# A conditioned decoder block in one kernel: order of the opening, place of the rotary tables, pace of the modulation, order at the second norm

## The chip, the cores and the metric

One NeuronCore of a Trainium2 chip runs the whole kernel. The metric is device time in microseconds. The engines are TensorE (PE, matmuls; PEld, its weight loads), VectorE (DVE), ScalarE (ACT), GpSimd (POOL) and SyncE (SP, which here only issues DMAs). Each engine works through its own queue in order; an instruction that waits holds up all that stands behind it on its queue.

## The reference

One decoder block on x of 256 tokens by 2048 channels, batch 1, float32 throughout:

```python
mod = (silu(c) @ ada_w + ada_b)            # 6 vectors of 2048: shift, scale, gate of mixer and of FFN
h = rmsnorm(x, norm_mix_g) * (1 + scale_m) + shift_m
x = x + gate_m * token_mix(h, cos, sin, ...)   # h @ w_in -> GLA and MLA branches, gated merge, @ w_out
h = rmsnorm(x, norm_ffn_g) * (1 + scale_f) + shift_f
x = x + gate_f * swiglu(h, ffn_w_in, ffn_w_down)
return rmsnorm(x, final_norm_g)
```

`cos` and `sin` are the rotary tables, from the positions. `ada_w` is 2048 x 12288: 100 MB that are multiplied with one vector only. The weights of the matmuls are read once each.

## The kernel before

**Matmuls.** float32 operands are split in two parts of reduced precision: `hi` is a copy on ACT (L111), `lo` the difference on DVE (L112), and each product is three matmuls (L170-172 or L180-182). Weights come in halves: 256 rows by 512 columns, 512 KB, loaded into a ring of raw buffers (`raw_tile`, six buffers plus what `more_raw` adds), split into `hi` and `lo` (three buffers each). A half gives twelve matmuls of 512 columns. After each half the program calls `tick()`.

**Modulation in the background.** `tick()` runs what is in `later`, then `background()`, which advances the generators in the list `bg` by `pace[0]` steps on the average, then one step of the attention lanes `ATT` and `GLA`. Two kinds of generator stand in `bg`: `ada_cols` (L247) takes the transposed weight of one block of 128 channels, loads four half rows of 512 KB and forms a dot product of each with the row `crow` on DVE; it ends with `modulate` (L318), which scales, shifts and splits a block of h. `ada_steps` (L270) loads 256 rows by 512 columns per step, eight steps, adds them up on DVE with two operations per step (L282, L284), and for three of the six vectors sums over partitions on GpSimd (L294); that is a ninth step. `background(1000)` at L871 runs whatever is left when the last block (`i == 3`) of the `w_out` product begins, as the FFN's norm needs those vectors.

**Stages.** Opening (L406-425): x is loaded, `crow` is broadcast with four matmuls, x is squared and transposed (`x_blocks`), the norm's factor goes through `rsqrt_mean` (eleven small DVE operations) and `rows_of` (two DVE operations, one broadcast matmul, one copy), and the blocks 0 and 1 are modulated. Then the projections: sixteen jobs (each 512 or 368 columns of `w_in`) in four rounds over the contraction (2, 4, 4 and 6 blocks of 128), while the background makes the next round's blocks of h. In round 4, after job 0, `rope_tables` (L382) makes the sine and cosine tables from the angles that `rope_angles` (L348) computes on GpSimd. Then the MLA heads in eight pairs together with three gate blocks and the GLA scores (56 ticks), the GLA output gate (L779, 32 ticks), `mla_wo` (L801, 32), `gla_wo` (L822, 32), `w_out` (L855, 32, of which 24 ahead of `i == 3`), the second norm (L897-911), the FFN (L923) and the last norm. There are 12 `ada_steps` generators between the heads and `w_out`.

**What sets the order.** The program is traced in order, but a planner, which simulates the engines, decides the order on each queue: the instruction that is ready first by its simulation goes first, so an instruction can stand far ahead of its place in the program. `keep_in_program_order(ins)` pins an instruction behind the one that was traced before it on its engine; `add_manual_dep(..., NoSync)` pins it behind a named one. Both set an order in a queue and add no wait by themselves. In the opening of before only the two loads of x are pinned.

**Lines to follow.** L407: loads of x. L408: `rope_angles`. L411-415: `crow`. L417: squares. L197-209: factor. L215-219: broadcast of the factor. L253: loads of the half rows, L256: dots. L321-323: `modulate`. L384-395: rotary tables. L728, L822, L855: paces. L871: the rest of the background. L888-890: residual add and square at `w_out`. L902-907: transposes and copies of the new x. L916, L917: two loads issued by GpSimd behind the norm.

Of the kernel before, what the change touches and what calls it, by code (L numbers as in the profile page):

```python
# [51 lines left out]
def tile_block(ctx: ExitStack, tc: tile.TileContext, x, positions, ada_w, ada_t, ada_b, w_in, gla_gk_w, gla_wo,  # L52
# [52 lines left out]
    def split_raw(raw, kk, cols, perm=None):  # L105
# [58 lines left out]
    def form_a(ps, w, ah, al, k0, first, last, cols, rows=(0, 1)):  # L164
        for kk, (hi, lo) in enumerate(w):
            k = k0 + kk
            for t in rows:
# [4 lines left out]
                T.matmul(ps[t][:, :cols], lhsT=al[:, k, ts], rhs=hi, start=False, stop=en)  # L172
# [22 lines left out]
    def rsqrt_mean(dst, ssq, n, w, eng=None):  # L195
        v, l = sb(w, "rv"), sb(w, "rl")
        V.tensor_scalar(out=v, in0=ssq, scalar1=1.0 / n, scalar2=EPS, op0=ALU.mult, op1=ALU.add)  # L197
        yi = dst.bitcast(I32)
        V.tensor_scalar(out=yi, in0=v.bitcast(I32), scalar1=-0.5, scalar2=float(0x5F3759DF), op0=ALU.mult, op1=ALU.add)
        for _ in range(3):  # L200
# [6 lines left out]
            V.tensor_tensor(out=l, in0=dst, in1=dst, op=ALU.mult)  # L207
            V.scalar_tensor_tensor(out=l, in0=l, scalar=-0.5, in1=v, op0=ALU.mult, op1=ALU.mult)
            V.scalar_tensor_tensor(out=dst, in0=l, scalar=1.5, in1=dst, op0=ALU.add, op1=ALU.mult)

    def rows_of(col, dst):
        ps = aux_bank()
        d = sb(S, "e", 3)
        for t in range(2):
            V.tensor_scalar(out=d[:, t * P:(t + 1) * P], in0=ident, scalar1=col[:, t:t + 1], scalar2=None, op0=ALU.mult)  # L215
# [31 lines left out]
    def ada_cols(k, now=False):  # L247
        for m in (1, 0):
            c = m * 16 + k
            part = sb(1, "md", 4)  # L250
            for hf in range(2):
                raw = raw_tile()
                nc.sync.dma_start(out=raw, in_=ada_t[m * D + k * P:m * D + (k + 1) * P, hf * 1024:(hf + 1) * 1024])  # L253

                def dot(raw=raw, hf=hf, c=c, part=part):
                    V.tensor_tensor_reduce(out=raw, in0=raw, in1=crow[:, hf * 1024:(hf + 1) * 1024], scale=1.0,  # L256
                                           scalar=part if hf else cb[:, c:c + 1], op0=ALU.mult, op1=ALU.add,
                                           accum_out=mod[:, c:c + 1] if hf else part)

                if now:  # L260
                    dot()
# [120 lines left out]
    def rope_tables(ang, ang2):  # L382
        four = sb(512, "sc", 2)
        V.scalar_tensor_tensor(out=ang2, in0=ang, scalar=-1.0, in1=ang, op0=ALU.mult, op1=ALU.max)  # L384
# [3 lines left out]
        for i, a in enumerate((ang, ang2)):  # L388
            A.copy(out=four[:, i * S:(i + 1) * S].rearrange("p (t r f) -> p t r f", t=2, r=4),
                   in_=a.rearrange("p (t f) -> p t f", t=2).unsqueeze(2).broadcast_to([P, 2, 4, 32]))  # L390
            for t in range(2):
                c = slice(i * S + t * P, i * S + (t + 1) * P)
                T.transpose(out=ps[:, c], in_=four[:, c], identity=ident)
        A.activation(out=sin_t, in_=ps[:, 0:S], func=AF.Sin, scale=sgn)
# [11 lines left out]
    for t in range(2):  # L406
# [642 lines left out]
```

## Time and profile before

| | us |
|---|---|
| median of 3 runs | 1770.57 (1770.28 to 1771.84) |
| profiled execution, its own time | 1769.9 |
| its span, first to last instruction | 1768.1 |
| TensorE busy | 1694.1 (96%) |
| DVE busy | 1235.1 (70%) |
| ACT busy | 832.2 (47%) |
| GpSimd busy | 121.2 (7%) |
| HBM traffic | 410.5 MB read, 6.3 MB written |

Busy shares are averages over the whole span. A timeline row reads: start, length, engine, line, operation, output and input tile with their shapes, count, and in brackets how long the engine had been idle before and what released it. A row with a count above 1 covers several instructions back to back. [...] In the code `s`, `raw`, `mm`, `aux` and so on are names of tiles; `s` stands for all large slots.

### The profile page before, as it was taken

Reading aid. Unit: us, or ns where it says so; the run is one execution under the profiler, and the core shown is the slowest. Engines: PE = TensorE matmul, PEld = TensorE weight load, DVE = VectorE, ACT = ScalarE, POOL = GpSimd, SP = SyncE. Lnnn points to the kernel's source line nnn. Section 1 sums busy time; section 2 is a strip of 40 time slices with the busy share of each in tenths; the row PEclk is TensorE's granted clock in tenths of the full one; section 3 lists DMA queues with packets and bytes.
Section 4 is the critical chain, followed back from the end, with each engine's and each line's share of the span. In section 5 each row is a group of like instructions: output and inputs, shape, how many; then the busy total and the mean of one; then the engine's idle time right before and its main releaser. Section 6 shows DMA issues by size and latency. Waiting matters only on the chain.

```text
span 1768.1 us, 23022 instructions
## 1 busy us (share of the span) xinstructions
PE 1694.1 (96%) x8388; PEld 1427.0 (81%) x8388; DVE 1235.1 (70%) x1797; ACT 832.2 (47%) x1154; POOL 121.2 (7%) x139
## 2 busy tenths in 40 slices
PE   4999999999999999999996799999999999999997
PEld 2998899889998887788884588888888888788885
DVE  5999977587786477999887767667664444555556
ACT  4644434356666555444442254444444444444443
POOL 5000000000000111110011100000000000000001
PEclk7999999999999999999998899999999999999999
DMA  8999986655545487999997658788786666555552
GB/s 300 355 349 322 322 249 195 187 190 150 171 117 187 158 297 242 357 367 317 323 345 261 238 155 273 236 251 270 237 248 189 189 191 190 178 190 187 187 186 108
DMA packets 196074, 418.31 MB, mean 237 GB/s; under 512 B 13060, under 2 KB 23636, under 8 KB 195320
## 3 DMA queue, kind: packets, MB, share of 16 engines
q1 hardware_dynamic: 194136, 410.27, 71.0%
q0 software_dynamic: 1680, 6.51, 1.0%
q8 instruction: 66, 1.08, 0.2%
q14 instruction: 48, 0.39, 0.1%
q10 hardware_dynamic: 144, 0.07, 0.0%
HBM read 410.49 MB, written 6.30 MB: 236 GB/s over the span
## 4 chain that ended last, share of the span: by engine, by line
PE 90%; DVE 4%; POOL 2%; issue 2%; DMA 1%; ACT 1%; DVEq 0%; ACTq 0%; POOLq 0%
PE mm L171 20%; PE mm L172 20%; PE mm L170 20%; PE mm L180 3%; PE mm L181 3%; PE mm L182 3%; PE mm L959 2%; PE mm L960 2%; PE mm L961 2%; PE gx L685 2%; PE gx L960 1%; PE aux L960 1%; PE aux L959 1%; PE gx L959 1%; PE aux L961 1%
## 5 line engine op out<-in xcount | busy, mean ns | idle before, releaser
L112 DVE TENSOR_TENSOR lo<-raw,hi 128x1024 fp32r<-128x1024 f32 (+3 forms) x518 | 599.7, 1163 | 356.6 <-ACT hi L111 354.3
L111 ACT CAST hi<-raw 128x1024 fp32r<-128x1024 f32 (+3 forms) x518 | 506.5, 984 | 567.6 <-PE mm L172 400.1
L171 PE MATMUL mm<-lo,s 128*128 128x512 f32 (+1 forms) x1648 | 647.1, 393 | 2.4 <-DVE lo L112 2.2
L172 PE MATMUL mm<-hi,s 128*128 128x512 f32 (+1 forms) x1648 | 640.9, 390 | 0.0
L170 PE MATMUL mm<-hi,s 128*128 128x512 f32 (+1 forms) x1648 | 587.1, 392 | 22.8 <-ACT hi L111 21.6
L170 PEld LDWEIGHTS mm<-hi,s 128*128 128x128 f32 x1648 | 310.3, 189 | 88.7 <-ACT hi L111 24.3
L171 PEld LDWEIGHTS mm<-lo,s 128*128 128x128 f32 x1648 | 311.8, 189 | 67.5 <-DVE lo L112 6.0
L172 PEld LDWEIGHTS mm<-hi,s 128*128 128x128 f32 x1648 | 311.7, 189 | 61.6 <-issue 0.7
L284 DVE SCALAR_TENSOR_TENSOR ada<-raw,cact,ada 128x512 f32<-128x512 f32 x191 | 143.0, 749 | 15.4 <-DMA raw<-in_ada_w_dram 12.8
L111 ACT CAST hi<-s 128x1024 fp32r<-128x1024 f32 (+1 forms) x65 | 67.5, 1039 | 114.5 <-PE mm L172 66.6
L180 PE MATMUL mm<-s,hi 128*128 128x256 f32 x416 | 118.5, 287 | 0.0
L181 PE MATMUL mm<-s,hi 128*128 128x256 f32 x416 | 117.4, 284 | 0.0
L182 PE MATMUL mm<-s,lo 128*128 128x256 f32 x416 | 115.4, 285 | 0.0
L112 DVE TENSOR_TENSOR lo<-s,hi 128x1024 fp32r<-128x1024 f32 (+1 forms) x65 | 80.3, 1236 | 32.0 <-ACT hi L111 31.6
L180 PEld LDWEIGHTS mm<-s,hi 128*128 128x128 f32 x416 | 79.6, 191 | 0.8 <-issue 0.3
L181 PEld LDWEIGHTS mm<-s,hi 128*128 128x128 f32 x416 | 79.6, 191 | 0.4
L182 PEld LDWEIGHTS mm<-s,lo 128*128 128x128 f32 x416 | 78.3, 191 | 0.0
L960 PE MATMUL mm<-lo,w 128*128 128x512 f32 x160 | 63.6, 398 | 0.0
L294 POOL PARTITION_ALL_REDUCE ada<-ada x12 | 45.2, 3763 | 269.5 <-DVE ada L284 269.5
L961 PE MATMUL mm<-hi,w 128*128 128x512 f32 x160 | 62.6, 393 | 0.0
L959 PE MATMUL mm<-hi,w 128*128 128x512 f32 x160 | 50.9, 396 | 0.7 <-ACT w L968 0.7
L968 ACT CAST w<-s 128x256 fp32r<-128x256 f32 x44 | 17.7, 408 | 59.1 <-PE aux L960 59.1
(274 smaller groups left out, 1694.4 us busy)
## 6 DMA issues: line engine op xcount, KB each, us to landing
raw<-in_ffn_w_in_dram SPq DMA_DIRECT2D x176, 512.0 KB, 4.5
raw<-in_w_in_dram SPq DMA_DIRECT2D x124, 512.0 KB, 4.9
raw<-in_ada_w_dram SPq DMA_DIRECT2D x102, 512.0 KB, 4.8
raw<-in_ffn_w_down_dram SPq DMA_DIRECT2D x88, 512.0 KB, 4.4
raw<-in_ada_t_dram SPq DMA_DIRECT2D x44, 512.0 KB, 5.9
s<-in_ada_w_dram SPq DMA_DIRECT2D x26, 512.0 KB, 6.7
s<-in_w_in_dram SPq DMA_DIRECT2D x23, 512.0 KB, 4.4
raw<-in_mla_wo_dram SPq DMA_DIRECT2D x20, 512.0 KB, 5.6
```

The costliest lines, as they stand in the source:

```text
L111: A.copy(out=hh_, in_=rr)
L112: V.tensor_tensor(out=ll_, in0=rr, in1=hh_.bitcast(F32), op=ALU.subtract)
L170: T.matmul(ps[t][:, :cols], lhsT=ah[:, k, ts], rhs=hi, start=st, stop=False)
L171: T.matmul(ps[t][:, :cols], lhsT=ah[:, k, ts], rhs=lo, start=False, stop=False)
L172: T.matmul(ps[t][:, :cols], lhsT=al[:, k, ts], rhs=hi, start=False, stop=en)
L180: T.matmul(o, lhsT=hi[:, pick], rhs=ah[:, k], start=st, stop=False, skip_group_check=True)
L181: T.matmul(o, lhsT=hi[:, pick], rhs=al[:, k], start=False, stop=False, skip_group_check=True)
L182: T.matmul(o, lhsT=lo[:, pick], rhs=ah[:, k], start=False, stop=en, skip_group_check=True)
L284: ins = V.scalar_tensor_tensor(out=acc, in0=raw[:, k - k0], scalar=c, in1=acc, op0=ALU.mult, op1=ALU.add)
L959: T.matmul(o, lhsT=ah[:, ts], rhs=hi[:, ns], start=first, stop=False)
L960: T.matmul(o, lhsT=ah[:, ts], rhs=lo[:, ns], start=False, stop=False)
L961: T.matmul(o, lhsT=al[:, ts], rhs=hi[:, ns], start=False, stop=last)
```

## The change

Four edits, in the order of the program.

1. **Opening.** The work keeps its parts and gets another order, which is pinned: `crow` first, then x's first half and its square, four half rows with their dots (block 0), x's second half and its square, two half rows with their dots, then the transposes of x, the factor and its diagonal with every DVE operation pinned, the last two half rows, then `rope_angles`, then the modulation of the blocks 0 and 1. `ada_cols` is cut in `ada_dots` and `ada_mod` for it.
2. **Rotary tables.** The first DVE operation, both copies, the four transposes and the first sine are pinned in program order, so behind the end of job 0 of round 4.
3. **Paces.** 0.2 to 0.4 for the heads, 0.65 to 0.8 for `gla_wo`, 0.6 to 0.75 for `w_out`.
4. **Second norm.** Transposes of x from column block 4 on are put behind the last matmul of `w_out`; of the next splits the first is free, the second and third have their `hi` copy behind the last square of the residual (`sqr`).

```diff
@@ split_raw, and a new list and helper
-            A.copy(out=hh_, in_=rr)
+            h = A.copy(out=hh_, in_=rr)
+            if fence:
+                follow(h, fence.pop(0))
...
+    fence = []
+
+    def follow(ins, prev):
+        if prev is not None:
+            tc.add_manual_dep(ins.ins, prev.ins.name, mybir.DependencyInfo(
+                mybir.DependencyClass.NoSync, mybir.DependencyReason.DATA), reason="order on one engine")
...
+    def rsqrt_mean(dst, ssq, n, w, eng=None, pinned=False):
...
+        pin = tc.keep_in_program_order if pinned else lambda i: i
...
+    def rows_of(col, dst, pinned=False):
...
-    def ada_cols(k, now=False):
+    def ada_dots(k, now=False):
...
                 if now:
-                    dot()
+                    tc.keep_in_program_order(d)
+                    tc.keep_in_program_order(dot())
...
         flush()
+
+    def ada_mod(k):
         V.scalar_tensor_tensor(out=mod[:, 16 + k:17 + k], in0=mod[:, 16 + k:17 + k], scalar=1.0, in1=nmg[:, k:k + 1],
                                op0=ALU.add, op1=ALU.mult)
         modulate(k, xTk, rx, 0, hhk, hlk)
+
+    def ada_cols(k):
+        yield from ada_dots(k)
+        ada_mod(k)
@@ rope_tables
-        V.scalar_tensor_tensor(out=ang2, in0=ang, scalar=-1.0, in1=ang, op0=ALU.mult, op1=ALU.max)
+        pin(V.scalar_tensor_tensor(out=ang2, in0=ang, scalar=-1.0, in1=ang, op0=ALU.mult, op1=ALU.max))
...
+        for i in range(4):
+            c = slice(i * P, (i + 1) * P)
+            pin(T.transpose(out=ps[:, c], in_=four[:, c], identity=ident))
+        pin(A.activation(out=sin_t, in_=ps[:, 0:S], func=AF.Sin, scale=sgn))
@@ opening
-    for t in range(2):
-        tc.keep_in_program_order(nc.sync.dma_start(out=xtok[:, t], in_=x[0, t * P:(t + 1) * P]))
-    ang, ang2 = rope_angles()
...
-        A.copy(out=crow[:, 512 * b:512 * (b + 1)], in_=ps)
+        pin(A.copy(out=crow[:, 512 * b:512 * (b + 1)], in_=ps))
+    more_raw((qk, 0, 4))
+    first = [ada_dots(k, True) for k in range(2)]
     for t in range(2):
-        A.activation(out=vt[:, 0:2048], in_=xtok[:, t], func=AF.Square, accum_out=sx[:, t:t + 1])
+        pin(nc.sync.dma_start(out=xtok[:, t], in_=x[0, t * P:(t + 1) * P]))
+        pin(A.activation(out=vt[:, 0:2048], in_=xtok[:, t], func=AF.Square, accum_out=sx[:, t:t + 1]))
+        for _ in range(4 - 2 * t):
+            next(first[t])
     for k in range(0, KT, 2):
         x_blocks(k)
-    rsqrt_mean(rc2, sx, D, 2)
-    rows_of(rc2, rx)
-    more_raw((qk, 0, 4))
+    rsqrt_mean(rc2, sx, D, 2, pinned=True)
+    rows_of(rc2, rx, pinned=True)
+    for _ in first[1]:
+        pass
+    for _ in first[0]:
+        pass
+    ang, ang2 = rope_angles()
     for k in range(2):
-        for _ in ada_cols(k, True):
-            pass
+        ada_mod(k)
@@ paces
-    pace[0] = 0.2
+    pace[0] = 0.4
-    pace[0] = 0.65
+    pace[0] = 0.8
-    pace[0] = 0.6
+    pace[0] = 0.75
@@ second norm
-                form_a(ps, w, k256(mh), k256(ml), k, False, k == KT - 2, 512, (t,))
+                last = form_a(ps, w, k256(mh), k256(ml), k, False, k == KT - 2, 512, (t,))
...
-            A.activation(out=u, in_=x1v[:, t, cs], func=AF.Square, accum_out=sq[:, j:j + 1])
+            sqr = A.activation(out=u, in_=x1v[:, t, cs], func=AF.Square, accum_out=sq[:, j:j + 1])
...
+                if k >= 4:
+                    follow(tp, last)
...
+    fence[:] = [None, sqr, sqr]
```

## Rows read from the trace of the kernel before

**Rows 1.** The page's part 1: busy time, share of the span, instructions.

```profile
PE 1694.1 (96%) x8388; PEld 1427.0 (81%) x8388; DVE 1235.1 (70%) x1797; ACT 832.2 (47%) x1154; POOL 121.2 (7%) x139
```

**Rows 2.** Busy time in two windows (us; count), then granted clock, DMA share, GB/s.

```profile
20.00:40.00 20.00, 3.30 (x9) 1.90 (x9) 11.12 (x26) 3.00 (x6) 14.73 (x30) 0.52 0.75 290
40.00:60.00 20.00, 19.35 (x83) 15.54 (x82) 19.59 (x28) 16.24 (x25) 0.00 (x0) 0.96 0.96 341
```

**Rows 3.** The same view, windows of the attention, `mla_wo`, `gla_wo` and `w_out` stages.

```profile
450.00:500.00 50.00, 49.93 (x348) 46.04 (x348) 38.72 (x105) 34.43 (x79) 1.58 (x3) 1.00 0.50 161
733.00:797.00 64.00, 64.00 (x284) 52.72 (x283) 59.95 (x85) 27.84 (x27) 7.30 (x2) 1.00 1.01 363
862.00:886.00 24.00, 24.00 (x111) 19.91 (x110) 22.25 (x36) 11.01 (x12) 0.61 (x1) 1.00 0.90 298
953.00:1007.00 54.00, 30.49 (x106) 21.96 (x104) 37.64 (x65) 12.99 (x17) 8.56 (x4) 0.75 0.68 239
```

**Rows 4.** Timeline around `w_out`'s last block: start us, us, engine, line, operation.

```profile
952.99 0.39 PE L172 MATMUL mm<-hi,s 128*128 128x512 f32 x1
...
1006.36 0.39 PE L172 MATMUL mm<-hi,s 128*128 128x512 f32 x1
...
1009.72 1.22 DVE L112 TENSOR_TENSOR lo<-raw,hi 128x1024 fp32r<-128x1024 f32 x1
...
1010.85 0.69 DVE L889 TENSOR_TENSOR s<-s,sc 128x512 f32<-128x512 f32 x1
...
1011.57 0.63 ACT L890 ACTIVATE sc<-s 128x512 f32<-128x512 f32 x1 [1.01 <-DVE s L889]
...
1017.63 0.80 PE L170 MATMUL mm<-hi,s 128*128 128x512 f32 x1 [1.12 <-ACT s L322]
```

**Rows 5.** Waits of PE and DVE, 0 to 60 us: total us, times, longest.

```profile
PE aux L393 <- ACT sc L389: 11.9, 1, 11.9
...
DVE s L384 <- POOL s L379: 6.5, 1, 6.5
```

**Rows 6.** Timeline of the opening; in brackets the idle time before, its releaser.

```profile
12.46 1.28 DVE L256 CUSTOM_DVE_ANT_0 raw<-raw,s,vec 128x1024 f32<-128x1024 f32 x1 [6.74 <-DMA raw<-in_ada_t_dram]
...
24.55 1.19 PE L216 MATMUL aux<-e,ones 128*128 128x256 f32 x2 [5.36 <-DVE e L215]
...
27.25 0.94 DVE L323 SCALAR_TENSOR_TENSOR s<-e,mod,s 128x256 fp32r<-128x256 f32 x2
...
36.90 0.24 POOL L379 TENSOR_SCALAR s<-s 128x64 f32<-128x64 f32 x1
...
38.58 1.22 PE L170 MATMUL mm<-hi,s 128*128 128x512 f32 x2 [0.26 <-ACT hi L111]
```

**Rows 7.** Waits of PE, 880 to 1040 us.

```profile
PE mm L170 <- ACT hi L111: 20.6, 3, 16.0
```

**Rows 8.** Timeline of the SP queue, 880 to 1010 us.

```profile
929.08 0.37 SPq L102 DMA_DIRECT2D s<-in_ada_w_dram  x1
...
957.74 6.67 SPq L102 DMA_DIRECT2D raw<-in_ada_w_dram  x5
```

**Rows 9.** DMA view, 0 to 80 us: GB/s in 40 slices of 2 us.

```profile
GB/s 17 303 401 402 144 358 422 412 418 405 401 394 405 398 397 406 389 107 0 4 156 265 336 291 360 418 398 393 397 393 406 401 387 385 389 354 339 328 266 383
```

**Rows 10.** Timeline: GpSimd steps beside a busy and an idle VectorE; a dot alone.

```profile
22.93 1.19 POOL L360 TENSOR_TENSOR s<-s 128x64 f32<-128x64 f32 x1
...
35.63 0.32 POOL L360 TENSOR_TENSOR s<-s 128x64 f32<-128x64 f32 x1
...
39.70 1.28 DVE L256 CUSTOM_DVE_ANT_0 raw<-raw,s,vec 128x1024 f32<-128x1024 f32 x1
```

**Rows 11.** Chain of work by time, 880 to 1040 us: start, us, what.

```profile
936.59 0.87 PE aux L905 x8
```

**Rows 12.** The page's part 5: busy us, mean ns of one, idle before.

```profile
L284 DVE SCALAR_TENSOR_TENSOR ada<-raw,cact,ada 128x512 f32<-128x512 f32 x191 | 143.0, 749 | 15.4 <-DMA raw<-in_ada_w_dram 12.8
```

**Rows 13.** The page's part 6: count, KB each, median us to landing.

```profile
raw<-in_ada_w_dram SPq DMA_DIRECT2D x102, 512.0 KB, 4.8
```

More of the change, by code (lines that the diff above doesn't have):

```diff
@@ L171, in form_a @@
                 T.matmul(ps[t][:, :cols], lhsT=ah[:, k, ts], rhs=lo, start=False, stop=False)
-                T.matmul(ps[t][:, :cols], lhsT=al[:, k, ts], rhs=hi, start=False, stop=en)
+                mm = T.matmul(ps[t][:, :cols], lhsT=al[:, k, ts], rhs=hi, start=False, stop=en)
+        return mm
     def form_b(ps, w, ah, al, k0, first, last, cols, blocks=None):
@@ L206, in rsqrt_mean @@
                 continue
[L207 to L211, printed above, removed]
+            pin(V.tensor_tensor(out=l, in0=dst, in1=dst, op=ALU.mult))
+            pin(V.scalar_tensor_tensor(out=l, in0=l, scalar=-0.5, in1=v, op0=ALU.mult, op1=ALU.mult))
+            pin(V.scalar_tensor_tensor(out=dst, in0=l, scalar=1.5, in1=dst, op0=ALU.add, op1=ALU.mult))
+    def rows_of(col, dst, pinned=False):
+        pin = tc.keep_in_program_order if pinned else lambda i: i
         ps = aux_bank()
@@ L214, in rows_of @@
         for t in range(2):
-            V.tensor_scalar(out=d[:, t * P:(t + 1) * P], in0=ident, scalar1=col[:, t:t + 1], scalar2=None, op0=ALU.mult)
+            pin(V.tensor_scalar(out=d[:, t * P:(t + 1) * P], in0=ident, scalar1=col[:, t:t + 1], scalar2=None,
+                                op0=ALU.mult))
         T.matmul(ps[:, :S], lhsT=ones, rhs=d, start=True, stop=True)
@@ L252, in ada_cols @@
                 raw = raw_tile()
-                nc.sync.dma_start(out=raw, in_=ada_t[m * D + k * P:m * D + (k + 1) * P, hf * 1024:(hf + 1) * 1024])
+                d = nc.sync.dma_start(out=raw, in_=ada_t[m * D + k * P:m * D + (k + 1) * P, hf * 1024:(hf + 1) * 1024])
                 def dot(raw=raw, hf=hf, c=c, part=part):
-                    V.tensor_tensor_reduce(out=raw, in0=raw, in1=crow[:, hf * 1024:(hf + 1) * 1024], scale=1.0,
-                                           scalar=part if hf else cb[:, c:c + 1], op0=ALU.mult, op1=ALU.add,
-                                           accum_out=mod[:, c:c + 1] if hf else part)
+                    return V.tensor_tensor_reduce(out=raw, in0=raw, in1=crow[:, hf * 1024:(hf + 1) * 1024], scale=1.0,
+                                                  scalar=part if hf else cb[:, c:c + 1], op0=ALU.mult, op1=ALU.add,
+                                                  accum_out=mod[:, c:c + 1] if hf else part)
                 if now:
-                    dot()
+                    tc.keep_in_program_order(d)
+                    tc.keep_in_program_order(dot())
                 else:
@@ L388, in rope_tables @@
         for i, a in enumerate((ang, ang2)):
-            A.copy(out=four[:, i * S:(i + 1) * S].rearrange("p (t r f) -> p t r f", t=2, r=4),
-                   in_=a.rearrange("p (t f) -> p t f", t=2).unsqueeze(2).broadcast_to([P, 2, 4, 32]))
-            for t in range(2):
-                c = slice(i * S + t * P, i * S + (t + 1) * P)
-                T.transpose(out=ps[:, c], in_=four[:, c], identity=ident)
-        A.activation(out=sin_t, in_=ps[:, 0:S], func=AF.Sin, scale=sgn)
+            pin(A.copy(out=four[:, i * S:(i + 1) * S].rearrange("p (t r f) -> p t r f", t=2, r=4),
+                       in_=a.rearrange("p (t f) -> p t f", t=2).unsqueeze(2).broadcast_to([P, 2, 4, 32])))
+        for i in range(4):
+            c = slice(i * P, (i + 1) * P)
+            pin(T.transpose(out=ps[:, c], in_=four[:, c], identity=ident))
+        pin(A.activation(out=sin_t, in_=ps[:, 0:S], func=AF.Sin, scale=sgn))
         A.activation(out=cos_t, in_=ps[:, S:2 * S], func=AF.Sin)
@@ L405, in tile_block @@
     sx, rc2 = sb(2, "sx"), sb(2, "rx")
-    for t in range(2):
-        tc.keep_in_program_order(nc.sync.dma_start(out=xtok[:, t], in_=x[0, t * P:(t + 1) * P]))
-    ang, ang2 = rope_angles()
+    pin = tc.keep_in_program_order
     for b in range(4):
```

11 lines of the change are left out of this document (5 added, 6 removed).

## The prediction

> **What bounds the kernel now.** I read the page first, then windows, waits and timelines of the stretches in which TensorE is not full. TensorE is busy in 96% of the span [rows 1]; what is left to win lies where it idles, and these places are few. The windows show two that matter. Between 20 and 40 us it works 3.30 of 20 us at a granted clock of 0.52, while the next window is full again [rows 2]. Between 953 and 1007 us it works 30.49 of 54 us at 0.75, while the middle stages around are at 100% [rows 3]. A third is the norm behind it: the last matmul ahead of the norm starts at 1006.36, the first FFN matmul at 1017.63 [rows 4].
>
> What holds each: in the opening, PE waited 11.9 us for a ScalarE copy and VectorE 6.5 us for GpSimd [rows 5]. The timeline gives the story: the broadcast of the norm's factor is on PE at 24.55, and the modulation could have followed, but both VectorE and ScalarE had a rotary step next in their queues, and those wait for the last GpSimd step of the angles, which starts at 36.90. The first weight split stands behind that copy on ScalarE, and the first projection matmul comes at 38.58 [rows 6]. At 953 PE waits 20.6 us, in three waits, for the first split of a `w_out` half [rows 7]: the SP queue issued sixteen modulation loads in a row, the first at 929.08, the last five from 957.74, with no `w_out` load between them [rows 8].
>
> **Part 1, the opening (L401-425).** The same loads and dots stay. What is removed is the rotary chain from the front: `rope_angles` comes later in program order and the tables' steps are pinned behind what precedes them in the trace of the program, which is the fourth round. GpSimd keeps its 25 us of small steps (40 by the code), now beside other work; behind them on its queue stand only the clearing of `krx` and the mask's cast (L485), wanted a stage later. On SP x's second half moves behind four half rows, and the first `w_in` load stays behind all eight. When can PE start? Ahead of the first matmul x (2.1 MB), eight half rows of modulation (4.2 MB) and constants (0.4 MB) must land. The moved bytes per 2 us slice [rows 9] add up to 3.3 MB at 12 us, 6.6 MB at 20 us and 7.4 MB at 22 us; the first dot began at 12.46 [rows 6] with about 3.4 MB moved where 3.0 were needed, so a load lands about 0.5 MB after its own bytes. In the new order x's second half lands near 16.3 us, its Square (2048 columns; 512 take 0.63 us [rows 4], so at most 2.5) ends by 18.8, the sixth half row lands near 18.9 and its dot (1.28 us) ends at 20.3. From there the pinned chain runs: eleven factor steps, diagonal, broadcast, modulation. The same chain at the later norm takes 6.78 us from the start of the residual add at 1010.85 to the matmul at 1017.63 [rows 4]; less the add and the Square (0.69 and 0.63 us), 5.4 us: 25.7. The two last dots stand between the diagonal and the modulation, 2.7 us, of which the broadcast's 1.2 us [rows 6] covers about half, and the extra copy of the row adds 0.4: first matmul at about 27.4 instead of 38.58, 11.2 us earlier. Bounds: 25.7, if the dots hide; 31, if VectorE is given three other operations of 1.2 us ahead of the modulation.
>
> Not all of that is kept. What is late next is supply. Before, buffers had filled by 36 us. Afterwards round 0 wants, per half (12 matmuls; 284 matmuls in 64 us, so 2.70 us [rows 3]), one weight load and 1.05 modulation loads, 1.07 MB, against about 0.8 MB per 2 us slice [rows 9], so 1.08 MB in 2.70 us: just enough. VectorE has per half a subtraction of 1.22 us [rows 4] and 1.05 dots of 1.28 plus a 0.08 read-out, 2.65 us, plus four modulations of two operations (the second takes 0.47 [rows 6]), about 0.95 us each, in sixteen halves: 2.9 of 2.70. It also starts two dots (2.7 us) behind where it stood before. I charge 2.5 us, between 0 (the next rounds' lower paces 0.55 and 0.7 take it up) and 4. Opening: **-9**, between -13 and -4.
>
> A rule that speaks against this part: GpSimd steps take 1.19 us while VectorE runs and 0.32 while it idles, yet the dot takes 1.28 us both beside them (12.46) and at 39.70, with GpSimd idle [rows 6, 10]. So here the waiting falls on GpSimd, whose result nobody wants before the fourth round. [...]
>
> **Part 2, the tables in round 4.** Four transposes of 0.11 us (eight take 0.87 [rows 11]) now stand in a full PE stream: +0.4. They wait for two VectorE steps pinned behind the accumulation of job 0 and for a copy on ScalarE. Queued behind: on PE the matmuls of the next job, on ScalarE its hi splits, three buffers deep. I take +0.5; the lower bound is 0.4, the upper 3, one split and one subtraction late.
>
> **Part 3, the paces.** A modulation step is a load and two VectorE operations of 0.749 us [rows 12]. There are twelve generators of nine steps, 108. Ticks times pace before: 56 x 0.2 + 32 x 0.6 + 32 x 0.8 + 32 x 0.65 + 24 x 0.6 = 91, so 17 are dumped at `i == 3`: 15 loads and 2 reductions, which is what the sixteen loads in a row show [rows 8] (one was regular). After: 56 x 0.4 + 19.2 + 25.6 + 32 x 0.8 = 92.8, and 24 x 0.75 = 18 ahead of `i == 3` covers the last 15.2. The dump is empty. Price of the dump: the eight halves of `i == 3` need 21.7 us and 0.9 of transposes; they took 53.4 (953.2 to 1006.6 [rows 3, 4]). **-31**. It can't give more; less if steps are left over.
>
> Where the work goes: 11 steps to the attention stage, where VectorE works 38.72 of 50 us and DMA half its share [rows 3]; 11 x 1.5 = 17 us in some 275: cover is there, and I cost it at nothing; without the cover it is the rival below. Five steps (6.4 us, and about 1 for reading a reduction) go to `gla_wo`, 90 us, where VectorE is at 22.25 of 24 us and DMA at 0.90 in the densest window; the stage ahead of it ran at pace 0.8 with VectorE 59.95 of 64, DMA 1.01, and PE still full [rows 3]. So pace 0.8 has been held once; the new stage adds eight evacuations more of 0.68 us. I charge +2, between 0 and 7 (all of it exposed). `w_out` gets the same number of steps, closer together.
>
> **Part 4, the norm.** Sixteen transposes (blocks of `i` 1 and 2) are held back behind the last matmul. Eight cost 0.87 us in PE's stream [rows 11]; those of `i == 2` fell into a gap that closes: 1.74 us leave the path (0.87 is in the -31), and run while VectorE and ScalarE work on the factor. The two later splits wait for the last Square, so a subtraction of 1.22 us as at 1009.72 [rows 4] no longer stands between multiply and add. From the last matmul's end to the FFN's first matmul it took 10.9 us; without the interposed subtractions and with the other half's evacuation done early it is 0.6 for the multiply plus 6.8: 7.4. Against that, two subtractions done ahead of time before now come later, and four more ScalarE copies of 0.6 us share the tail: I give back 1 us. **-3.5** with the transposes; bounds -6 (PE also keeps its clock) and +1 (both subtractions fall into the factor chain, which is not pinned here).
>
> **Sum.** -9 + 0.5 - 31 + 2 - 3.5 = -41. The profiled execution took 1769.9 us, of which 1768.1 are span; the median is 1770.57, 0.7 us more. 1769.9 - 41 = 1728.9; **1729**. Its own range by the bounds is 1720 to 1738.
>
> **Rivals.**
> 1. The dump's gain is partly given back: `gla_wo` and `w_out` become bound by VectorE or DMA. For it: 22.25 of 24 us before five more steps. Against: pace 0.8 held in the stage ahead. All 7 us exposed there and as much again in `w_out`: 1741.
> [...]
> 3. Slower: in the attention stage the ring has six raw buffers and feeds 7 weight loads in each 7 ticks. If every added step exposes its landing (4.8 us [rows 13]) and its two operations, 11 x 6.3 = 69 us, the kernel ends at 1798. It decides from 41 / 6.3 = 7 exposed steps of 11. Against: the steps already there left PE full [rows 3].
> 4. It doesn't do what it says: steps are left at `i == 3` (the count has a margin of 2.8 steps), or the planner that orders the queues bunches the loads anyway. Then about two thirds of the dump stay: 1750.
>
> **How the numbers follow.** Forecast 0.62; rival 1 0.14; rival 2 0.12; rival 3 0.05; rival 4 0.07. The likeliest is 1729. The range takes the forecast's own and rivals 1 and 2: 1719 to 1745, which leaves out 0.12 and some misjudged size. This kernel's time can be told from no change by about 0.2%, 3.5 us. Faster 0.94, within 0.01 (rival 3 at about 7 exposed steps), slower 0.05.
>
> **What would show it.** Part 1: no rotary step in the first 60 us of PE, first projection matmul near 27 us, the window 20 to 40 with 12 us or more of PE work; wrong if PE then waits for splits. Part 2: four transposes of `four` after the first job of round 4 with no wait above 1 us. Part 3: no modulation load behind the last `w_out` block's, that block in about 22 us, PE full in the attention stage and `gla_wo`. Part 4: transposes right after the last matmul, 7 to 8 us to the FFN's first matmul. A PE share in the middle stages under 97%, or a `w_out` block above 25 us, would make the number wrong.

## The result and the profile after

The changed kernel takes 1750.86 us (median of 4 runs, 1748.45 to 1751.26) where the kernel before took 1770.68 beside it: a ratio of 0.9884, interval 0.9867 to 0.9901. That is 20 us less; 41 were forecast, and 1750.86 lies above the range. Of all the runs below one execution, the profiled one of the last kernel, was slow (4011.68 us) and is left out of its median. The profiled execution of the changed kernel took 1751.26 us with a span of 1749.5, 18.6 less than the span before.

To see where the 18.6 come from and go to, the start of one and the same evacuation is read from the timelines of both kernels at the end of each stage. The difference (after less before) runs:

```
stage ends with                            before     after     after - before   forecast so far
first evacuation of round 0                 42.8      35.5         -7.3            -9
round 4, the twelfth job of sixteen        349.9     343.1         -6.7            -8.5
attention stage and O_G                    702.8     698.4         -4.4            -8.5
first evacuation of mla_wo                 732.5     739.9         +7.4            -8.5
w_out, block i == 2                        953.4     965.6        +12.2            -6.5
w_out, block i == 3                       1008.5     987.4        -21.1            (-37.5)
first FFN gate behind the norm            1039.7    1020.8        -18.9            -41
last evacuation of the kernel             1757.2    1738.6        -18.6            -41
```

The dump is gone, as forecast, and the opening came near its term. But between that job of round 4 and the last `w_out` block the kernel loses 19 us that the forecast put at 2, and most of them, 12, around the start of `mla_wo`. (Line numbers are those of the changed kernel where its rows are shown, up to 29 above those of before.) The page of after has TensorE at 97% where it was 96% [rows 1]:

```profile
PE 1698.6 (97%) x8388; PEld 1429.3 (82%) x8388; DVE 1231.9 (70%) x1797; ACT 829.9 (47%) x1154; POOL 129.5 (7%) x139
```

The windows answer [rows 2, 3] (busy us and count of PE, PEld, DVE, ACT and POOL, then granted clock, the share of full speed that TensorE was allowed, DMA share, GB/s). The opening's window has 13.77 us of TensorE work for 3.30; the end of `w_out` (953 to 987: the later half of block `i == 2` and the whole of `i == 3`) is full; the windows of `mla_wo` and `gla_wo`, full before, have each lost about 0.5 us, with their stages 7 to 12 us later than before:

```profile
20.00:40.00 20.00, 13.77 (x48) 10.11 (x47) 19.26 (x42) 11.01 (x18) 18.09 (x24) 0.66 1.03 395
40.00:60.00 20.00, 20.00 (x96) 16.77 (x95) 19.12 (x27) 16.52 (x25) 5.01 (x6) 1.00 1.03 389
...
733.00:797.00 64.00, 63.48 (x272) 51.54 (x273) 58.71 (x88) 26.80 (x29) 7.48 (x2) 0.97 0.93 327
862.00:886.00 24.00, 23.47 (x106) 18.58 (x105) 22.24 (x29) 10.24 (x12) 0.00 (x0) 1.00 0.98 337
953.00:987.00 34.00, 34.00 (x151) 28.10 (x150) 21.94 (x30) 12.94 (x15) 4.17 (x3) 1.00 0.70 253
```

The opening's timeline answers [rows 6]: the broadcast stands at 24.14, the first modulated columns at 25.52 (VectorE) and 26.09 (ScalarE), no rotary step among them. Then the first split (L111) idles 2.21 us for its load, and the first projection matmul comes at 30.30 instead of 38.58:

```profile
24.14 0.70 PE L229 MATMUL aux<-e,ones 128*128 128x256 f32 x2 [0.16 <-ACT s L362]
25.52 0.93 DVE L341 SCALAR_TENSOR_TENSOR e<-s,mod,s 128x256 f32<-128x256 f32 x2
26.09 0.91 ACT L342 ACTIVATE s<-e,mod 128x256 fp32r<-128x256 f32 x2 [0.83 <-DVE e L341]
29.20 1.04 ACT L111 CAST hi<-raw 128x1024 fp32r<-128x1024 f32 x1 [2.21 <-DMA raw<-in_w_in_dram]
30.30 1.22 PE L179 MATMUL mm<-hi,s 128*128 128x512 f32 x2 [5.45 <-ACT hi L111]
```

On the SP queue the last modulation load ahead of the FFN now stands at 933.24, and behind 949 there are only weights and one short row of the mixer's gate (at 967.63), where before sixteen modulation loads stood in a row [rows 8]:

```profile
933.24 0.37 SPq L102 DMA_DIRECT2D raw<-in_ada_w_dram  x1
...
949.32 7.07 SPq L102 DMA_DIRECT2D raw<-in_w_out_dram  x4
957.15 2.85 SPq L102 DMA_DIRECT2D raw<-in_ffn_w_in_dram  x2
```

And here are the 12 us. GpSimd's timeline at the start of `mla_wo` (in brackets the idle time before, and its releaser; "issue" means that nothing the profile shows was awaited). L213 to L216 are the twelve small steps of the factor of the last gated head, 0.2 us each; after the third of them the planner of the queues has put an all-reduce of the modulation (L314). GpSimd idles 9.18 us before it and 7.23 us behind it:

```profile
709.12 0.20 POOL L214 TENSOR_TENSOR rl<-rl,rv 128x2 f32<-128x2 f32 x1
709.40 0.19 POOL L215 TENSOR_SCALAR rl<-rl 128x2 f32<-128x2 f32 x1
718.77 3.25 POOL L314 PARTITION_ALL_REDUCE ada<-ada  x1 [9.18 <-issue]
729.25 0.18 POOL L216 TENSOR_TENSOR gr<-gr,rl 128x2 f32<-128x2 f32 x1 [7.23 <-issue]
```

The waits of DVE and PE from 690 to 745 us (total, times, longest) say who stood behind it. VectorE waits 6.6 us for the reduced row and 6.4 for the factor; a lower half of a weight is queued behind the first of these, and TensorE waits 6.0 us for it and 2.8 for the factor's product. That is 8.8 of the 11.8 us; in the two windows from 720 to 740 us (shown with the factors on VectorE below) the granted clock was 0.66 and 0.83, and how much of the rest is due to that was not separated:

```profile
DVE ada L321 <- POOL ada L314: 6.6, 1, 6.6
DVE s L786 <- POOL gr L216: 6.4, 1, 6.4
...
PE mm L180 <- DVE lo L114: 6.0, 1, 6.0
PE gx L795 <- DVE s L786: 2.8, 2, 2.4
```

The norm's timeline answers [rows 4]: last `w_out` matmul 986.79, first FFN matmul 997.87, 11.08 us where it was 11.27. Two subtractions of the splits (L114) stand between the factor's steps on VectorE:

```profile
986.79 0.40 PE L181 MATMUL mm<-hi,s 128*128 128x512 f32 x1
...
991.28 0.16 DVE L219 SCALAR_TENSOR_TENSOR rl<-rl,rv 128x2 f32<-128x2 f32 x1
991.41 1.23 DVE L114 TENSOR_TENSOR lo<-raw,hi 128x1024 fp32r<-128x1024 f32 x1
992.56 0.15 DVE L220 SCALAR_TENSOR_TENSOR rx<-rl,rx 128x2 f32<-128x2 f32 x1
992.63 1.22 DVE L114 TENSOR_TENSOR lo<-raw,hi 128x1024 fp32r<-128x1024 f32 x1
...
994.93 0.48 DVE L227 TENSOR_SCALAR e<-ident,rx 128x128 f32<-128x128 f32 x2
...
997.87 0.79 PE L179 MATMUL mm<-hi,s 128*128 128x512 f32 x1 [1.11 <-ACT s L342]
```

### The profile page after: what moved, and what is told of

The parts are those of the page before. It is cut to its first block, busy times and chain, and to the rows that moved or that the text cites. A ratio compares the mean times of both kernels' runs of the same rounds, so it can differ in the third digit from the quotient of the medians.

```text
span 1749.5 us, 23029 instructions
## 1 busy us (share of the span) xinstructions
PE 1698.6 (97%) x8388; PEld 1429.3 (82%) x8388; DVE 1231.9 (70%) x1797; ACT 829.9 (47%) x1154; POOL 129.5 (7%) x139
## 4 chain that ended last, share of the span: by engine, by line
PE 85%; DVE 6%; DMA 4%; issue 3%; ACT 2%; POOL 0%; SPq 0%; DVEq 0%; ACTq 0%; POOLq 0%
PE mm L180 19%; PE mm L181 19%; PE mm L179 19%; PE mm L190 3%; PE mm L191 3%; PE mm L192 3%; PE mm L988 2%; PE mm L989 2%; PE mm L990 2%; DVE lo L114 2%; PE gx L711 1%; PE gx L989 1%; PE aux L989 1%; PE gx L988 1%; PE aux L988 1%
## 5 line engine op out<-in xcount | busy, mean ns | idle before, releaser
L114 DVE TENSOR_TENSOR lo<-raw,hi 128x1024 fp32r<-128x1024 f32 (+3 forms) x520 | 597.8, 1156 | 349.4 <-ACT hi L111 344.8
L111 ACT CAST hi<-raw 128x1024 fp32r<-128x1024 f32 (+3 forms) x520 | 507.9, 984 | 567.8 <-PE mm L181 419.4
L111 ACT CAST hi<-s 128x1024 fp32r<-128x1024 f32 (+1 forms) x63 | 65.1, 1036 | 96.0 <-PE mm L181 38.2
L114 DVE TENSOR_TENSOR lo<-s,hi 128x1024 fp32r<-128x1024 f32 (+1 forms) x63 | 78.8, 1251 | 31.3 <-ACT hi L111 31.1
L314 POOL PARTITION_ALL_REDUCE ada<-ada x12 | 45.9, 3826 | 262.3 <-DVE ada L304 253.1
```

The lines of the kernel that those rows point to most:

```text
L111: h = A.copy(out=hh_, in_=rr)
```

## The experiments

**Theory:** the change does what it says; the missing 20 us are mostly one thing, an all-reduce between two small steps of GpSimd, which pays for a change of kind in both directions (the 9.18 and 7.23 us of idle time above). **Rivals:** the faster pace is simply too much for VectorE and the loads; or the loss belongs to the earlier opening, which shifts the whole plan. First the parts alone, and one repair. Differences below are of the same evacuations as in the table above.

### The opening alone

```diff
 change, with these lines as before:
+    pace[0] = 0.2      # attention
+    pace[0] = 0.65     # gla_wo
+    pace[0] = 0.6      # w_out
-    fence[:] = [None, sqr, sqr]
-                if k >= 4: follow(tp, last)
```

> The opening and the pinned rotary tables alone: the three paces and the order at the norm are those of the kernel before. From the two traces, matmul by matmul: the change gained 7.2 us at the first projection matmul (30.30 for 38.58 us), held that to the last round of the latents, and lost 5 us again between the latents and the heads. Theory A: that loss belongs to the paces, not to the opening, so this kernel keeps 6 to 8 us: 1763 to 1765. Rival B: the loss comes from the opening or the rotary tables themselves (a shifted queue): 1767 to 1769. The prediction on record had 9 us less 0.5 for these two parts: 1762.

Measured: 1764.1 us, ratio 0.9965 (0.9951 to 0.9979). The difference to the kernel before is -7.3 at the first evacuation, -6.8 behind the rotary tables in round 4, -7.3 at the end of O_G and -6.4 from there to the last `w_out` block. At the end of this trace it is -5.0, and the medians differ by 6.1. Theory A holds: the opening gives 7 at its place, the tables cost 0.5 (the difference steps from -7.3 to -6.8 where they stand), and neither causes the losses; 0.9 at the start of `mla_wo` comes with the opening.

### The paces alone

```diff
 kernel before:
-    pace[0] = 0.2
+    pace[0] = 0.4
...
-    pace[0] = 0.65
+    pace[0] = 0.8
...
-    pace[0] = 0.6
+    pace[0] = 0.75
```

> The kernel before with the three paces of the change (0.4, 0.8 and 0.75 for 0.2, 0.65 and 0.6) and nothing else. The prediction on record: 31 us gained at the dump in the last block of w_out, 2 lost elsewhere, so 1741 to 1742. Theory A from the ledger of the two traces: 33 gained at the dump, 12 lost at the start of mla_wo, 5 before the heads, about 5 in small pieces in the output projections: 1756 to 1760. Rival B: the 12 us come from the shift of the whole schedule by the earlier opening, so that paces alone don't show them: 1744 to 1748.

Measured: 1755.74 us, ratio 0.9922 (0.9908 to 0.9937), 14.5 less. Difference to the kernel before: -1.2 at the twelfth job of round 4, +1.5 at the end of O_G (between +1.7 and +6.0 at the evacuations of the heads' projections), +13.7 at the first evacuation of `mla_wo`, +18.3 ahead of the last block, -14.4 behind the norm. So all three losses come with the paces, and the 12 us among them need no earlier opening. Theory A, 0.3 under its range; the forecast on record for this part, 1741 to 1742, missed by 14.

### The norm alone

```diff
 kernel before:
+    fence[:] = [None, sqr, sqr]            # splits behind the squares
+                if k >= 4: follow(tp, last)    # transposes behind the last matmul
```

> The kernel before with the order of splits and transposes at the norm alone (no change of paces or opening). The prediction on record: 3.5 us gained (bounds: 6 gained, 1 lost), 1767. Theory A from the trace of the changed kernel: the two subtractions that come early fall between the steps of the factor on VectorE and take back what the earlier split gives; 0 to 2 lost: 1770.5 to 1773. Here the block before the norm still carries the dumped modulation steps, so a result beyond 1767 or 1773 would say that the norm's wait isn't set by these orders at all.

Measured: 1770.78 us, ratio 1.0004 (0.9995 to 1.0013): nothing. The timelines show two opposite effects: the last evacuation of `w_out` comes 1.8 us earlier against the block ahead of it, and the first FFN gate gives 1.9 back. The forecast's 3.5 fell.

### The all-reduce held to its place

```diff
 change:
-            G.partition_all_reduce(ar, acc, ...)
+            tc.keep_in_program_order(G.partition_all_reduce(ar, acc, ...))
```

> The changed kernel, with GpSimd's all-reduces of the modulation held to their place in the program, so that none stands between the steps of a factor of the gated heads (in the changed kernel one stands between the eleventh and twelfth step of one factor, and GpSimd idles 9.2 us ahead of it and 7.2 us behind it). Theory A: the 12 us that the changed kernel loses at the start of mla_wo are those two switches, in a chain that the matmuls wait for: 1738 to 1741. Rival B: the loss is load, too many modulation steps on VectorE and the DMA queue in that stage whatever the place of the all-reduce: 1749 to 1752. In between: a switch is still paid, at a place where only part of it is hidden.

(By the rows of the change the all-reduce stands between the third and fourth of the twelve steps, not the eleventh and twelfth.)

Measured: 1744.39 us, ratio 0.986 (0.9845 to 0.9875), 6.5 less than the change: the case in between. The factor now runs through, but the same all-reduce comes 8.02 us behind its last step, with nothing awaited, and VectorE's reads of it stand in its queue already. GpSimd's timeline, then the waits of PE and DVE, 690 to 745 us:

```profile
714.61 0.20 POOL L216 TENSOR_TENSOR gr<-gr,rl 128x2 f32<-128x2 f32 x1
722.82 3.25 POOL L314 PARTITION_ALL_REDUCE ada<-ada  x1 [8.02 <-issue]
```

```profile
PE mm L180 <- DVE lo L114: 5.2, 1, 5.2
...
DVE ada L321 <- POOL ada L314: 5.9, 1, 5.9
```

One of the two idle stretches is gone and the other is still waited for. That fits the theory, but load on VectorE could still claim the rest.

### The factors on VectorE

```diff
 change:
-        rsqrt_mean(r, st, GDV, 2, G)
+        rsqrt_mean(r, st, GDV, 2)
```

> The changed kernel with the gated heads' factors worked out on VectorE (11 small instructions for GpSimd's 12), so that GpSimd has nothing but all-reduces in that stage. With the all-reduce held to its place (the run before this) 5.2 us of TensorE's wait for a lower half were left at the start of mla_wo, behind VectorE's wait of 5.9 us for an all-reduce that began 8.0 us after the factor's last step. Theory A: those 8.0 us are GpSimd's change from one kind of work to the other, so here both are gone: 11 to 12.5 us less than the changed kernel, 1738 to 1740. Rival B: what was left is the load of that stage and the small steps on VectorE add to it: 1744 or more.

Measured: 1738.22 us, ratio 0.9819 (0.9804 to 0.9833), 12.6 less than the change. All of it at one place: the difference to the change is +1.0 at the end of O_G, -13.1 at the first evacuation of `mla_wo`, -13.0 at the end. The all-reduce starts at 709.17 now, 0.2 us after the sum on VectorE that it reads (708.26 and 0.75 long), and TensorE waits 1.1 us in that stretch instead of 8.8. That row, then the windows of the change, then of this kernel:

```profile
709.17 3.23 POOL L314 PARTITION_ALL_REDUCE ada<-ada  x1 [44.35 <-DVE ada L304]
```

```profile
720.00:730.00 10.00, 5.42 (x12) 3.81 (x12) 3.20 (x12) 0.75 (x1) 2.60 (x4) 0.66 0.54 180
730.00:740.00 10.00, 7.25 (x29) 5.88 (x29) 8.31 (x13) 2.25 (x6) 1.16 (x6) 0.83 0.36 110
```

```profile
720.00:730.00 10.00, 10.00 (x50) 8.38 (x49) 10.00 (x16) 3.71 (x6) 0.00 (x0) 1.00 1.02 371
730.00:740.00 10.00, 8.94 (x38) 6.71 (x38) 9.78 (x12) 5.06 (x5) 0.00 (x0) 1.00 0.93 322
```

VectorE does more here (nine small steps more for each head; two of the eleven stood there already) and TensorE is fuller: load was not the cause. Rival B falls.

### One small all-reduce put into the kernel before

```diff
 kernel before, last gated head, behind the factor's third step:
+    pin(G.partition_all_reduce(sb(w, "rz"), l, channels=P, ...))   # 128x2, result unused
```

> The kernel before with one added all-reduce of 128x2 elements (its result is not used), put between the third and fourth GpSimd step of the last gated head's factor, the place where the changed kernel has a 128x512 one. Nothing else differs. Theory A: GpSimd pays for the change of kind in both directions whatever the size, about 9 us ahead of the small all-reduce and 7 behind it, and TensorE loses most of what exceeds the cover: 9 to 13 us at the start of mla_wo, 1779 to 1784. Rival B: the changed kernel's loss there came from the order of VectorE's work and not from GpSimd: the small all-reduce costs its own few us beside other work, 1770 to 1773.

Measured: 1785.4 us, ratio 1.0085 (1.007 to 1.01), 15 more; theory A, and more than its upper end. The all-reduce itself takes 0.40 us, the idle stretches are about as long as in the change:

```profile
714.95 0.19 POOL L204 TENSOR_SCALAR rl<-rl 128x2 f32<-128x2 f32 x1
723.97 0.40 POOL L204 PARTITION_ALL_REDUCE rz<-rl  x1 [8.83 <-issue]
731.98 0.18 POOL L205 TENSOR_TENSOR gr<-gr,rl 128x2 f32<-128x2 f32 x1 [7.60 <-issue]
```

VectorE waits 14.6 us for the factor and TensorE 13.8 behind it, at a granted clock that falls to 0.50 in the next window; the difference to the kernel before is +0.1 at the end of O_G and +15.3 at the first evacuation of `mla_wo`, 17.2 after it. The waits from 690 to 760 us, then the windows:

```profile
DVE s L760 <- POOL gr L205: 18.7, 2, 14.6
...
PE gx L769 <- DVE s L760: 14.0, 2, 13.8
```

```profile
720.00:730.00 10.00, 1.44 (x7) 0.85 (x5) 0.00 (x0) 4.06 (x4) 0.40 (x1) 0.73 0.73 270
730.00:740.00 10.00, 4.59 (x15) 3.72 (x16) 5.58 (x7) 0.95 (x2) 1.75 (x9) 0.50 0.17 50
```

So the price is that of the change of kind, not of the reduction's size (8.83 and 7.60 us of idle time around 128x2, 9.18 and 7.23 around the change's 128x512), and no more modulation steps are needed for it. Nor is it a price of every all-reduce: in the run before, where the gated heads leave GpSimd nothing but all-reduces, the one at 709.17 follows another all-reduce, behind 44.35 us of idle time, and starts 0.2 us after its operand, as the later ones ahead of the norm do in the kernel before (0.16 to 0.17 us, behind 23 to 38 us of idle time). With the run before, the 12 us are shown.

In the rows these stretches are idle time with nothing awaited, 8.0 to 9.2 us into the all-reduce and 7.2 to 7.6 on the way back. What GpSimd does in them no row here shows.

### The subtractions at the norm, moved twice

`late` does for the subtraction of a split what `fence` does for its copy: it puts it behind a named operation.

```diff
 change (first run); change with the factors on VectorE (second run):
+    late[:] = [None, last_diag, last_diag]     # first: behind the products with the identity
+    late[:] = [None, mods[1][1], mods[2][1]]   # second: behind the 2nd and 3rd modulated column
```

> The changed kernel with the second and third subtraction of the split ahead of the FFN held behind the last of the two products with the identity on VectorE (they stood between the steps of the factor). Theory A: the factor chain shrinks by the two, 2.4 us, and the first FFN matmul comes 1.9 to 2.4 us earlier: 1748 to 1749. Rival B: the first FFN matmul is bound by the copies and the modulated columns, or by these same subtractions one step later: no change, 1750 to 1751.

Measured: 1751.13 us, as the change: by the median rival B, in its second form. The timeline tells more than the median can: from the last `w_out` matmul to the first FFN matmul 9.80 us instead of 11.08. The chain did shrink, but both subtractions now stand, 2.35 us long, ahead of the first modulated column:

```profile
992.35 0.48 DVE L227 TENSOR_SCALAR e<-ident,rx 128x128 f32<-128x128 f32 x2
992.75 2.35 DVE L114 TENSOR_TENSOR lo<-raw,hi 128x1024 fp32r<-128x1024 f32 x2
995.02 1.26 DVE L341 SCALAR_TENSOR_TENSOR e<-s,mod,aux 128x256 f32<-128x256 f32 x3
```

1.3 us are less than the medians can tell (about 0.2%, 3.5 us); by the timeline the theory's mechanism is there with somewhat over half of its price. Hence the second place:

> The changed kernel with the factors on VectorE (1738.2) and the second and third subtraction at the norm held behind the second and third modulated column of the FFN's input (in the run that held them behind the products with the identity they stood ahead of the first modulated column, and 1.4 us were gained there in the trace). Theory A: the first FFN matmul comes 2 to 2.6 us earlier than with the subtractions inside the factor: 1735.6 to 1736.5. Rival B: matmuls then wait for those lower halves a little later, and no more than 1 us is kept: 1737 to 1738.

Measured: 1734.41 us, ratio 0.9793 (0.978 to 0.9807), 3.8 less than with the factors on VectorE alone and under the range of theory A. The stretch is 9.12 us, and the difference to that kernel goes from -1.8 ahead of the norm to -4.4 behind it: 2.6 belong to the norm, as theory A had it; the 1.8 arose ahead of the norm, as the plan of the queues shifted, and are no merit of the edit.

### Only the transposes at the norm

```diff
 change with the factors on VectorE:
-    fence[:] = [None, sqr, sqr]
```

> The changed kernel with the factors on VectorE (1738.2), and at the norm only the order of the transposes, not that of the splits, which are as before the change. Theory A from the traces with the norm's order alone: the transposes behind the last matmuls end those 1.8 us earlier, and the splits behind the squares lose 1.9 of it again, as their subtractions then fall into the factor's chain; so here 1 to 2 us are gained: 1736.2 to 1737.2. Rival B: the splits' order is what lets the factor begin early (without it two copies of 1.0 us stand ahead of the last square on ScalarE), and it loses what the subtractions had cost: 1738 to 1739.5.

Measured: 1735.68 us, ratio 0.9802 (0.9789 to 0.9816), 2.5 less than with the factors on VectorE, which the medians can't tell from nothing. The stretch is 9.02 us; in the trace the difference to that kernel goes from -2.7 to -4.5 over the norm: 1.8 gained there, theory A. The 2.7 arose ahead of the norm, where this edit does nothing. So, by these traces, of the two orders that the change brings to the norm the transposes help and the splits cost, about as much.

### The start of the attention stage

```diff
 change:
-    pace[0] = 0.4
+    pace[0] = 0.2
     for pr in range(8):
-        mla_pair(pr, between)
+        mla_pair(pr, between); pace[0] = 0.43
```

> The changed kernel with the pace of the attention stage 0.2 until its first pair is through, as before the change, and 0.43 behind that, so that about as many steps as in the changed kernel are run by the stage's end. Theory A: the 5 us that the changed kernel loses between the latents and the first pair come from the modulation's steps put ahead of the last accumulations of the gates: 4 to 5 us come back, 1746 to 1747 (unless the planner sets the all-reduces otherwise against the gated heads' factors, which is to be read from the trace). Rival B: any added step costs alike, wherever it stands: 1750 to 1751.

Measured: 1751.12 us, as the change: rival B by the median. The trace of the change had shown the steps ahead of the last accumulations of the gates, a late spill (L579), and a copy that waits for it; GpSimd's and ScalarE's rows:

```profile
385.40 0.53 POOL L579 DMA_DIRECT2D ga_sp<-s  x1 [10.21 <-DVE s L499]
...
390.46 0.58 ACT L647 COPY s<-mm 128x512 f32<-128x512 f32 x1 [1.90 <-DMA ga_sp<-s]
```

Here the first pair does come 5.8 us earlier than in the change, but by the end of O_G 0.7 of it is left. From the twelfth job of round 4 to the end of O_G the stage loses 1.1 us against the kernel before, where the change loses 2.3 and the paces alone 2.7; the place of the steps is worth about 1 us there, and nothing that the medians show.

### The first projection half

```diff
 change with the factors on VectorE:
-    background(2)
+    turn[0] += RAW; pace[1] += 2       # its buffer is free from the start; the two steps run later
...
-        ada_mod(k)
+        lead[:] = [ada_mod(k)[1]] * 4; late[:] = lead[:1]   # dots and its subtraction behind the columns
```

> The changed kernel with the factors on VectorE (1738.2) and one more edit at the opening: the first projection half takes a buffer that is free from the start, the two modulation steps that stood ahead of it are run after it, and the split's subtraction and the next four dot products stand behind the first two modulated columns. Theory A: the first projection matmul at 30.30 us waits for that half's load (the split idles 2.2 us for it); here it starts at 27.0 to 27.8 us and 2 to 3 us are kept to the end: 1735 to 1736.5. Rival B: the loads and VectorE are both full until 45 us, so an earlier first matmul only waits later: under 1 us kept, 1737.5 to 1738.5.

Measured: 1735.66 us, ratio 0.9797 (0.9782 to 0.9812): theory A by the median, 2.6 less than with the factors on VectorE, though the medians can't tell that from nothing. The first projection matmul starts at 26.45, earlier than theory A had it, but then waits for its lower half:

```profile
26.45 0.73 PE L179 MATMUL mm<-hi,s 128*128 128x512 f32 x2 [2.26 <-ACT s L342]
28.50 0.55 PE L180 MATMUL mm<-lo,s 128*128 128x512 f32 x1 [1.32 <-DVE lo L114]
```

The difference to the kernel with the factors on VectorE is -4.2 at the first evacuation, -4.1 at the end of round 0, -2.8 in round 4, and -1.5 at the end: the gain is kept through the opening, 1.3 of it are gone by round 4 and 1.3 more in the output projections. So the change's opening was held by an order and not by the bandwidth (from 20 to 40 us 398 GB/s were moved here and 395 in the change, with 16.03 us of TensorE work for 13.77); the edit moves a load, two steps and VectorE's operations at once, and how much of it is the load's place alone was not run.

### Both edits together

> Both edits of the two runs before this at once, with the factors on VectorE. If what each gains stays, the sum: 1733 to 1734.5 (theory A on both); with one of the two failing 1735 to 1736.5; with both failing 1737.5 to 1738.5. The loss of the attention stage (3 us) and of the three output projections (5 us) to the added modulation steps is still in it.

Measured: 1732.0 us (median of four, 1731.07 to 1733.01), ratio 0.9779 (0.9766 to 0.9793); no trace of one of these four is kept. The two gains add up about as the sum said, 1 us under its range. It is 19 us under the change and 39 under the kernel before.

## Why the prediction was wrong

**The opening.** Right in mechanism, 7.2 for 9. The first projection matmul came at 30.30 for 27.4, inside the bounds of 25.7 to 31, and the modulated columns stood in time for it (25.52 and 26.09). What failed is "the first `w_in` load stays behind all eight": by place it did, but three more modulation loads and two later halves (at 11.11 and 13.66) stand ahead of the half that is wanted first, which the chain of the forecast did not hold. The SP queue behind the eight, that half last:

```profile
12.40 0.34 SPq L266 DMA_DIRECT2D w<-in_ada_t_dram  x1
...
16.24 1.60 SPq L266 DMA_DIRECT2D raw<-in_ada_t_dram  x2
18.78 0.38 SPq L102 DMA_DIRECT2D raw<-in_w_in_dram  x1
```

Of the 2.5 us for the supply behind it 1 was needed (8.3 at the first matmul, 7.3 at the first evacuation); the window 40 to 60 is full.

**GpSimd beside VectorE.** GpSimd's steps ran beside VectorE until 45 us. The ten dots beside them took 1.27 to 1.40 us, most near 1.34, and 1.28 once GpSimd was done: some 0.06 us more a dot, 0.6 in all, where the sum had no term. The cost fell nearly all on GpSimd, whose steps of 0.32 us [rows 10] took up to 1.39 there. Rival 2 (the opening gives nothing, 1738) fell: it gave 7.2.

**The tables in round 4.** 0.5 forecast, 0.5 measured (-7.3 to -6.8 with the opening alone).

**The dump.** Right: 31 forecast, 33.3 measured over the last block (+12.2 to -21.1), 32.4 with the paces alone. No step was left over.

**Where the work goes.** This is the step that failed: "+2, between 0 and 7", and the attention stage at nothing. It measured 2.3 in the attention stage and O_G, 11.8 at the start of `mla_wo`, and 4.8 from there to the last block, 18.9 in all. In the table's terms the forecast missed by 22 us: 16.9 of them here, 5.7 at the norm (2.2 lost where 3.5 were to be gained) and 1.7 in the opening, while the dump gave 2.3 more than its term. The forecast costed a step as a load and two operations of VectorE, and put the other queues at nothing; the third instruction of a generator, the all-reduce on GpSimd, was mentioned as "about 1 for reading a reduction". Moved earlier by the faster pace, one of them fell between the factor's steps in GpSimd's queue. In the kernel before the same changes of kind were there, but TensorE waited behind none of them. Most stood in idle stretches long enough to hide them: at 630.86 GpSimd had been idle for 15.55 us between two kinds, and its all-reduce started 0.14 us after VectorE's sum. One was not hidden, and the trace of before names it. The factor's start value was ready at 684.31, GpSimd's first step on it began at 688.28, and VectorE waited for the factor:

```profile
688.28 0.19 POOL L202 TENSOR_TENSOR rl<-gr 128x2 f32<-128x2 f32 x1 [7.84 <-DVE lo L112]
...
691.57 1.41 DVE L760 SCALAR_TENSOR_TENSOR s<-gx,gr,s 128x512 f32<-128x512 f32 x2 [4.02 <-POOL gr L205]
```

TensorE stayed busy through that, so the wait cost nothing, and the forecast had no term for what a change costs out of cover. Rival 1 had the sign and nearly the size of this loss (12 above the forecast), but put it on VectorE and the loads of `gla_wo` and `w_out`; there it was 4.8, and its own place was GpSimd's order.

**The 4.8 and the 2.3.** Shown to come with the paces (nothing of them with the opening alone, +4.6 and +2.7 with the paces alone). Why added steps cost about that much, VectorE at 93 of 100 us (800 to 900) or the buffers of the ring, stays open; TensorE's waits there are single ones of up to 1.0 us for a lower half.

**The norm.** -3.5 forecast, nothing measured alone; beside the paces it cost 1.6 (from `i == 2` to the first FFN gate the change gains 31.1, the paces alone 32.7; from the last `w_out` matmul to the first of the FFN it is 11.08 us in the change and 8.76 with the paces alone). The bound named for it, "both subtractions fall into the factor chain, which is not pinned here", is what happened. The forecast should have taken that end: the planner puts an operation where its operands are ready, and the edit made them ready just as the chain ran.

The forecast had named "A PE share in the middle stages under 97%" as what would make the number wrong; 720 to 730 us had 54%.

## What to carry to other kernels

When steps are moved in time, list every queue that they use, and for each queue ask what it will stand between; an engine that is busy 7% of the span can still hold the matmuls for 12 us. GpSimd's small elementwise steps and its all-reduces are best not mixed on a path that is waited for: here nine small steps on VectorE did what twelve on GpSimd did, for 12.6 us less. Look for such changes in the trace before, too: an idle stretch of GpSimd between two kinds can bear another engine's name as its releaser (7.84 us put down to VectorE here). A term that has one bound in an order that nothing pins should be taken at that bound, or the order be pinned.

## What the runs showed of the hardware

Where the profile shows nothing awaited, GpSimd's change from elementwise steps to an all-reduce took 8.0 to 9.2 us (8.02 with the all-reduce held, 8.83 with the small one, 9.18 in the change), back 7.2 to 7.6 (7.23 in the change, 7.60 with the small one), whether the all-reduce was 128x2 (0.40 us) or 128x512 (3.25 us). It can be shorter: behind the last factor of the kernel before an all-reduce began 6.78 us after the last step, 0.8 us after its operand. In the change one behind 6.82 us of idle time after such steps began 0.14 us after its operand, as did one behind 15.55 us in the kernel before: no price of the change of kind shows there. With the factors on VectorE an all-reduce that followed another one, behind 44.35 us of idle time, began 0.2 us after its operand. After TensorE's wait of 13.8 us behind the small all-reduce, the granted clock of the ten microseconds from 730 on was 0.50 (1.00 in the same window of the kernel before), and the loss (17.2 us by the evacuations, 16.9 by the spans) was more than the wait.
